# First operands of the down product in a two-level Strassen SwiGLU: loads and splits moved to a list of steps

## The chip, the core and the metric

The kernel runs on one core of a Trainium2 chip. Five engines work on their own instruction queues: PE (TensorE, matrix products), DVE (VectorE, elementwise work), ACT (ScalarE, activations and copies), POOL (GpSimd) and SP (SyncE, which here only issues transfers). The metric is the device time of one execution in microseconds (us); times below are medians of several executions of the same kernel.

## The reference, cut to what matters

Two layers over a residual stream of 1024 positions by 1024 channels. Layer 0 mixes with a short gated convolution, layer 1 with dilated attention; after each stands a SwiGLU feed-forward block, and a norm ends the whole. The part that this case is about is the feed-forward block, which runs twice:

```python
h = rms_norm(x, ffn_norm[i])
x = x + (jax.nn.silu(h @ w_gate) * (h @ w_up)) @ w_down    # 1024 -> 2816 -> 1024, all float32
```

## The kernel before, in words

**Precision.** A float32 product is made of three matmuls on a reduced type: an operand t is split into a high part (ACT rounds it, line 138 for weights, line 518 for activations) and a low part, t minus the high part (DVE, line 139 or 519); then high times high, high times low and low times high are added up in PSUM (lines 526 to 528). So every operand costs one ACT instruction, one DVE instruction, and three matmuls per use. Splits of activations are made by `hi` (line 516): it issues the ACT instruction at once and hands back a function that issues the DVE instruction.

**Strassen.** Products are done by the Strassen-Winograd scheme: seven products numbered 1 to 7 in place of eight, in the order `WINOGRAD = (1, 2, 6, 5, 7, 3, 4)`, over sums of quarters of the operands. For gate and up, the weights come in units of 256 columns; even unit numbers are gate, odd ones are up, 22 units in all (0 to 21). In units from 5 on, the products 2 and 4 of an even and an odd unit are done together with a second Strassen level, as seven "deep" products with numbers above 10 (`DEEPER = 10`), run with the odd unit. A product of the first level (`mm`, line 521) is 12 matmuls on 512 columns; a deep product (`deeper`, line 607) is 12 matmuls on 256 columns, whose results DVE adds to saved tiles (line 536).

**The order of the units.** It is written out by hand in `unit_order`, as a list of pairs (unit, product). `products` (line 554) walks through it, does the product at place n, and then calls `filled(n)` (in `run`, line 777), where other work is hung in. The last thirteen places, 168 to 180, are

```python
(21, 1) (20, 3) (21, 6) (21, 5) (21, 7) (21, 11) (21, 12) (21, 15) (21, 16) (21, 3) (21, 17) (21, 13) (21, 14)
```

**What comes after.** A finished pair of units gives four tiles of the hidden activations. `store` writes the Strassen sums of nine such pairs to DRAM tiles `parts[q, m]` (pair q, product m). The down product (`down`, line 741) reads them back: it works on chunks of three pairs (c = 0, 3, 6), and per chunk twice (n = 0 and n = 4) through the seven products, each with two blocks of 9 matmuls on 512 columns (k = n and k = n + 2); after each block DVE adds the bank to the residual stream X (line 747). After the two blocks of a product it calls `next(feed, None)`.

**The feed.** For a chunk, `feed` (line 715) is a generator whose step for product m loads the three tiles `parts[c + k, m]` into half pages named `hin` (line 723, on SP's queue) and then splits the three tiles that the step before loaded (ACT line 518, DVE line 519), into pages named `b`. For the first chunk its steps run at the places 176 to 180 of the unit order (the condition on line 791, the call on line 792) and then in `down`, after its products 1, 2 and 6: so product 1 is loaded at place 176 and split at place 177, product 2 split at 178, 6 at 179, 5 at 180, and 7, 3 and 4 within the down product.

**Queues and buffers.** Each engine runs its instructions in the order of the program. SP issues all weight loads (`raw`, line 152), the `hin` loads and the loads of X from its spilled copy (line 713, `load_x`) in program order too, each as soon as its buffer is free. Weights are split some products ahead (`take`, `ensure`). Half pages (128x512) come from a pool of 20, pages (128x1024) from a pool of 41, and PSUM has 8 banks; a new tile gets the place that has been free for the longest time, and its first writer waits for the last reader of the tile before.

Of the kernel before, what the change touches and what calls it, by code (L numbers as in the profile page):

```python
# [29 lines left out]
WINOGRAD = (1, 2, 6, 5, 7, 3, 4)  # L30
DEEP, DEEPER = (2, 4), 10
# [63 lines left out]
def trunk(ctx: ExitStack, tc: tile.TileContext, x, gains_in, cwi, ck, cwo, wqkv, wo, relb,  # L95
          wg, wu, wd, oneh, ident, out):
    nc = tc.nc
# [11 lines left out]
    def half_page(name, dt=F32):  # L109
        return scope["pool"].tile([128, 512], dt, name=name, tag="half", bufs=scope["halves"])  # L110
# [34 lines left out]
    ops, made, op_state = [], {}, [0, 0]  # L145
# [13 lines left out]
    def ensure(upto):  # L159
        while op_state[0] < min(upto + 1, len(ops)):  # L160
            key = ops[op_state[0] + 1][0] if op_state[0] + 1 < len(ops) else None
            if key in sums_of:
                sums_of.pop(key)()
            made[op_state[0]] = ops[op_state[0]][1]()
            op_state[0] += 1
# [49 lines left out]
    def add_deep(unit, key, u, rows, upto):  # L215
# [27 lines left out]
        def early(op):  # L243
            w = op()
            run(*[sums_of(j, m) for j, m in enumerate(DEEP)])
            return w
# [105 lines left out]
    def run(*gens):  # L352
        for _ in zip(*gens):
            pass
        for g in gens:
            for _ in g:
                pass
# [6 lines left out]
    def both(w, ks, acts):  # L364
        banks = two_banks()
        run(product(w, ks, acts, banks))
        return banks
# [126 lines left out]
    class Strassen:  # L494
# [215 lines left out]
        def load_x(self, *ns):  # L710
            for n in ns:
                X[n] = page("x")
                nc.sync.dma_start(X[n], self.source[n])

        def feed(self, c):

            tiles = None
            for m in WINOGRAD + (None,):
                new = None
                if m:  # L720
                    new = [half_page("hin") for k in range(self.chunk)]
                    for k in range(self.chunk):
                        nc.sync.dma_start(new[k], self.parts[c + k, m])
                if tiles:
                    lows = [self.hi(last, k, t, nc.vector)
                            for k, t in enumerate(tiles)]
                    for lo in lows:
                        lo()
                tiles, last = new, m
                if m:  # L730
                    self.b[m] = [None] * self.chunk
                    yield

        def feed_last(self, fs=None):
            for f in fs or self.plain:
                t = page("hin")
                nc.sync.dma_start(t, self.plain[f])
                self.hid[f] = split(t)
                yield

        def down(self, c, n, feed):

            p, r = {}, {}
            later = {2: (1,), 6: (3,), 5: (4,), 7: (6,), 3: (5,), 4: (7,)}

            def add(n, h, b):
                nc.vector.tensor_tensor(out=X[n][:, half(h)], in0=X[n][:, half(h)], in1=b, op=ALU.add)  # L747

            for m in WINOGRAD:
                for k in (n, n + 2):  # L750
                    if m == 1:
                        p[k] = bank()
                    if m == 5:
                        r[k] = bank()
                    b = bank() if m == 2 else r[k] if m in (3, 5) else p[k]
                    self.mm((c, k), m, b, m in (1, 2, 5), 4)
                    add(k + (m in (5, 7, 4)), int(m in (6, 5, 7, 3)), b)
                next(feed, None)
                if c == n == 0:
                    self.load_x(*later.get(m, ()))  # L760
                    self.rest(m)
# [10 lines left out]
        def run(self, start, hooks={}):  # L772

            self.base = op_state[1]
            last = self.nu - 1

            def filled(n):
                start(n)
                if self.key != CONV:
                    self.now = n + 1  # L780
                    i = self.order.index((3, 4))
                    if n == i - 10:
                        prep.append(self.deepen(2))
                    if n == i - 1:
                        prep.append(self.deepen(4))
                    for p in prep:
                        next(p, None)
                if self.key == CONV:
                    self.below(n, last)
                else:  # L790
                    if self.order[n][0] == last and n >= self.at(last, DEEPER + 6) - self.base:
                        next(feed, None)
                    if self.order[n] == (last, DEEPER + 7):
                        self.load_x(0, 2)
                        ensure(self.at(last, DEEPER + 4) + 4)
                self.idle(n)

            prep = []
            if self.key == CONV:
                self.products(filled, hooks)  # L800
                self.first_tiles()
                return
            feed = self.feed(0)
            self.products(filled, hooks)
            for c in range(0, self.pairs, self.chunk):
                self.down(c, 0, feed)
                feed = self.feed(c + self.chunk) if c + self.chunk < self.pairs else self.feed_last()
                self.down(c, 4, feed)
            run(feed)


    class Conv(Strassen):
# [148 lines left out]
        def first_tiles(self):  # L961

            run(self.low)
            upper = self.halved(range(CO, KT))
            for n in range(KT):
                banks = two_banks()
                run(product(take(("co", 0, n), 2), range(CO), self.hid, banks))
                if n + 2 < KT:
                    self.load_x(n + 2)
                add_to_x(n, banks)  # L970
                self.step(4 if n < 2 else None)
                if n >= 3:
                    next(upper, None)
            run(upper)
            for f in range(CO):
                del self.plain[f]
# [876 lines left out]
```

## Time and profile before

| what | before |
|---|---|
| median of 3 executions (lowest, highest) | 2205.99 us (2205.42, 2206.07) |
| span of the profiled execution, first to last instruction | 2203.1 us |
| ACT busy | 1000.5 us (45%) |
| POOL busy | 170.7 us (8%) |
| transfers, mean over the span | 119 GB/s |

The profiled execution shows no time of its own beside its span; the span ends 2.9 us below the median of the others. The two feed-forward blocks reach their last unit at about 749 us and 1940 us of the span. The busy time of PE counts overlapped matmuls once; waits are idle times of an engine before an instruction, with what released it. In a row of the timeline the columns are the start, the length, the engine, the line, the operation, the tile written and the tiles read, the size and the count of merged instructions.

### The profile page before, as it was taken

How to read it: one execution, taken by the hardware profiler on the slowest of the kernel's cores; microseconds unless marked ns; L12 is line 12 of the kernel's file. 1: busy time of each engine (PE TensorE's matmuls, PEld its weight loads, DVE VectorE, ACT ScalarE, POOL GpSimd, SP SyncE). 2: the span in 40 equal slices, each digit the busy share in tenths (PEclk: the TensorE clock that was granted, in tenths of full speed). 3: DMA queues.
4: the chain of work that ended last, by engine and by line, in shares of the span. 5: the costliest groups of instructions: out<-in, count | busy, mean ns of one | idle time of the engine just before them, and what ended most of it. 6: DMA issues, size and time to landing. Idle time of an engine off the chain costs nothing. (4 is left out here: it accounts for less than half of the span.)

```text
span 2203.1 us, 30573 instructions
## 1 busy us (share of the span) xinstructions
PE 2138.2 (97%) x11138; PEld 1825.5 (83%) x11138; DVE 1752.9 (80%) x3229; ACT 1000.5 (45%) x1812; POOL 170.7 (8%) x224
## 2 busy tenths in 40 slices
PE   7899999999999999999999999998999999999998
PEld 6788888778888878878999998886778888888887
DVE  7797758988888798865677777866888888889886
ACT  6433426434444444445455455534544444454435
POOL 0000001100101000010111111112000101000000
PEclk9999999999999999999999999998999999999999
DMA  4122543223323384323333333446223233366432
GB/s 155 55 86 71 210 153 87 96 91 100 116 96 120 117 281 144 119 68 131 91 91 92 94 97 90 152 154 170 77 77 102 105 105 111 96 226 204 158 91 77
DMA packets 135345, 261.89 MB, mean 119 GB/s; under 512 B 48328, under 2 KB 59608, under 8 KB 135194
## 3 DMA queue, kind: packets, MB, share of 16 engines
q1 hardware_dynamic: 75978, 184.80, 26.3%
q0 software_dynamic: 18048, 52.03, 7.0%
q10 hardware_dynamic: 41168, 23.10, 3.5%
q8 instruction: 88, 1.44, 0.3%
q14 instruction: 63, 0.52, 0.1%
HBM read 187.31 MB, written 66.27 MB: 115 GB/s over the span
## 5 line engine op out<-in xcount | busy, mean ns | idle before, releaser
L526 PE MATMUL bank<-b,w 128*128 128x512 f32 x1784 | 704.6, 395 | 25.6 <-DVE part L536 6.4
L528 PE MATMUL bank<-b,w 128*128 128x512 f32 x1784 | 700.4, 393 | 8.9 <-DVE w L139 8.9
L527 PE MATMUL bank<-b,w 128*128 128x512 f32 x1784 | 701.4, 393 | 0.0
L526 PEld LDWEIGHTS bank<-b,w 128*128 128x128 f32 x1784 | 338.6, 190 | 102.6 <-ACT part L532 7.4
L528 PEld LDWEIGHTS bank<-b,w 128*128 128x128 f32 x1784 | 338.7, 190 | 84.2 <-DVE w L139 13.1
L527 PEld LDWEIGHTS bank<-b,w 128*128 128x128 f32 x1784 | 338.7, 190 | 69.2 <-issue 0.7
L138 ACT ACTIVATE w<-combo 128x512 fp32r<-128x512 f32 (+2 forms) x464 | 234.5, 534 | 281.5 <-DVE combo L186 275.5
L139 DVE TENSOR_TENSOR w<-combo,w 128x512 fp32r<-128x512 f32 (+2 forms) x464 | 260.9, 576 | 57.5 <-ACT w L138 55.2
L532 ACT ACTIVATE part<-bank 128x512 f32<-128x512 f32 x168 | 99.5, 593 | 269.7 <-PE bank L528 258.6
L139 DVE TENSOR_TENSOR w<-raw,w 128x512 fp32r<-128x512 f32 (+2 forms) x316 | 169.4, 561 | 15.6 <-ACT w L138 14.1
L536 DVE TENSOR_TENSOR part<-part,bank 128x256 f32<-128x256 f32 (+1 forms) x348 | 159.1, 488 | 26.4 <-PE bank L528 14.2
L138 ACT ACTIVATE w<-raw 128x512 fp32r<-128x512 f32 (+2 forms) x316 | 150.7, 519 | 46.0 <-PE bank L528 11.2
L747 DVE TENSOR_TENSOR x<-x,bank 128x512 f32<-128x512 f32 x168 | 114.6, 682 | 30.7 <-PE bank L528 30.7
L347 PE MATMUL bank<-w_hi,w 128*128 128x512 f32 (+1 forms) x320 | 121.3, 379 | 4.4 <-ACT w L138 4.4
L349 PE MATMUL bank<-w_hi,w 128*128 128x512 f32 (+1 forms) x320 | 119.3, 373 | 0.9 <-DVE w L139 0.9
L348 PE MATMUL bank<-w_lo,w 128*128 128x512 f32 (+1 forms) x320 | 119.0, 372 | 0.0
L459 DVE TENSOR_TENSOR x<-x,bank 128x512 f32<-128x512 f32 (+1 forms) x104 | 66.1, 643 | 65.6 <-PE bank L349 57.3
L186 DVE TENSOR_TENSOR combo<-raw 128x512 f32<-128x512 f32 (+1 forms) x160 | 103.2, 645 | 4.0 <-DMA raw<-in_conv_w_in 4.0
L347 PE MATMUL bank<-h_hi,w_hi 128*128 128x512 f32 x256 | 104.6, 408 | 0.0
L349 PE MATMUL bank<-h_hi,w_lo 128*128 128x512 f32 x256 | 100.2, 391 | 0.7 <-DVE w_lo L139 0.7
L348 PE MATMUL bank<-h_lo,w_hi 128*128 128x512 f32 x256 | 99.9, 390 | 0.0
L1130 ACT ACTIVATE part<-part 128x512 f32<-128x512 f32 x66 | 39.7, 628 | 107.5 <-DVE part L536 107.5
(252 smaller groups left out, 3842.7 us busy)
## 6 DMA issues: line engine op xcount, KB each, us to landing
hin<-part SPq DMA_DIRECT2D x126, 256.0 KB
raw<-in_ffn_w_gate SPq DMA_DIRECT2D x44, 512.0 KB
raw<-in_ffn_w_up SPq DMA_DIRECT2D x44, 512.0 KB
part<-sum POOLq DMA_DIRECT2D x72, 256.0 KB, 2.7
raw<-in_ffn_w_down SPq DMA_DIRECT2D x48, 384.0 KB
x<-spill SPq DMA_DIRECT2D x24, 512.0 KB
raw<-in_attn_w_qkv SPq DMA_DIRECT2D x24, 512.0 KB
raw<-in_conv_w_in SPq DMA_DIRECT2D x21, 512.0 KB
```

Source lines behind the costliest of these rows:

```text
L138: nc.scalar.activation(hi, src, AF.Copy)
L139: eng.tensor_tensor(out=lo, in0=src, in1=hi, op=ALU.subtract)
L186: eng.tensor_tensor(out=c, in0=a, in1=b, op=op)
L347: nc.tensor.matmul(b, whi[:, a], ahi[:, s], start=first, stop=False)
L348: nc.tensor.matmul(b, whi[:, a], alo[:, s], start=False, stop=False)
L349: nc.tensor.matmul(b, wlo[:, a], ahi[:, s], start=False, stop=last)
L526: nc.tensor.matmul(b, hi[:, a], bhi, start=start and k == 0, stop=False, skip_group_check=True)
L527: nc.tensor.matmul(b, hi[:, a], blo, start=False, stop=False, skip_group_check=True)
L528: nc.tensor.matmul(b, lo[:, a], bhi, start=False, stop=k == n - 1, skip_group_check=True)
L532: nc.scalar.activation(t, b, AF.Copy)
L536: nc.vector.tensor_tensor(out=t, in0=t, in1=b, op=ALU.add)
L747: nc.vector.tensor_tensor(out=X[n][:, half(h)], in0=X[n][:, half(h)], in1=b, op=ALU.add)
```

## The change

In the feed-forward blocks, `feed` is taken apart into two functions, `load(m)` and `made(m)` (the split), and the first chunk gets a list of 17 steps of its own, `feed_first`. Its steps run from place 168 of the unit order on, after the last unit's first product; 13 of them lie in the units, four after the products 1, 2, 6 and 5 of the first pass of the down product. A pair (l, s) in the list means: split product s, then load product l. The other chunks' order is as before.

```diff
+        def feeding(self, c):
+
+            tiles = {}
+
+            def load(m):
+                tiles[m] = [half_page("hin") for k in range(self.chunk)]
+                for k, t in enumerate(tiles[m]):
+                    nc.sync.dma_start(t, self.parts[c + k, m])
+
+            def made(m):
+                self.b[m] = [None] * self.chunk
+                lows = [self.hi(m, k, t) for k, t in enumerate(tiles.pop(m))]
+                for lo in lows:
+                    lo()
+
+            return load, made
+
         def feed(self, c):
 
-            tiles = None
-            for m in WINOGRAD + (None,):
-                new = None
+            load, made = self.feeding(c)
+            for m, last in zip(WINOGRAD + (None,), (None,) + WINOGRAD):
                 if m:
-                    new = [half_page("hin") for k in range(self.chunk)]
-                    for k in range(self.chunk):
-                        nc.sync.dma_start(new[k], self.parts[c + k, m])
-                if tiles:
-                    lows = [self.hi(last, k, t, nc.vector)
-                            for k, t in enumerate(tiles)]
-                    for lo in lows:
-                        lo()
-                tiles, last = new, m
+                    load(m)
+                if last:
+                    made(last)
                 if m:
-                    self.b[m] = [None] * self.chunk
                     yield
+
+        def feed_first(self):
+
+            load, made = self.feeding(0)
+            for loads, mades in ((1, 0), (0, 0), (2, 0), (0, 1), (0, 0), (0, 2), (0, 0), (6, 0), (0, 0), (0, 6), (5, 0),
+                                 (0, 0), (0, 0), (7, 5), (3, 7), (4, 3), (0, 4)):
+                if mades:
+                    made(mades)
+                if loads:
+                    load(loads)
+                yield
...
-                    if self.order[n][0] == last and n >= self.at(last, DEEPER + 6) - self.base:
-                        next(feed, None)
+                    if n >= self.order.index((last, 1)):
+                        next(feed)
...
-            feed = self.feed(0)
+            feed = self.feed_first()
```

Laid beside the order of the units, the splits of the first chunk move so:

| operands of product | split before, after place | split in the changed kernel, after place |
|---|---|---|
| 1 | 177, (21, 3) | 171, (21, 5) |
| 2 | 178, (21, 17) | 173, (21, 11) |
| 6 | 179, (21, 13) | 177, (21, 3) |
| 5 | 180, (21, 14) | down product 1 |
| 7 | down product 1 | down product 2 |
| 3 | down product 2 | down product 6 |
| 4 | down product 6 | down product 5 |

The loads stand at the places 168 (product 1), 170 (2), 175 (6) and 178 (5), and after down products 1 (7), 2 (3) and 6 (4); before, they stood at 176, 177, 178, 179, 180 and after down products 1 and 2.

## The prediction, made before the result was known

> **What bounds the kernel now.** I read the page first, then the busy times by stage around the last unit of the first layer (the two feed-forward blocks are called layers here), then the timelines of PE, DVE, ACT and SP there.
>
> ```profile
> span 2203.1 us, 30573 instructions
> ...
> PE 2138.2 (97%) x11138; PEld 1825.5 (83%) x11138; DVE 1752.9 (80%) x3229; ACT 1000.5 (45%) x1812; POOL 170.7 (8%) x224
> ```
>
> PE is busy for 97% of the span: only its waits and its slow stretches can be won. The stages (columns: stretch, its length, busy us of PE, PEld, DVE, ACT, POOL, granted PE clock, DMA share, GB/s):
>
> ```profile
> 740.00:768.00 28.00, 28.00 (x150) 24.24 (x150) 20.79 (x45) 13.45 (x30) 1.62 (x3) 1.00 0.34 112
> 768.00:776.00 8.00, 6.23 (x42) 5.54 (x40) 7.38 (x18) 5.95 (x14) 0.54 (x1) 1.00 1.01 347
> 776.00:784.00 8.00, 7.76 (x33) 6.69 (x34) 7.97 (x18) 4.00 (x8) 0.00 (x0) 0.79 1.04 403
> 784.00:792.00 8.00, 6.55 (x30) 5.12 (x29) 7.97 (x15) 4.20 (x10) 1.08 (x2) 1.00 0.96 328
> ```
>
> From 740 to 768 PE never waits and DVE idles for 28.00 - 20.79 = 7.2 us. From 768 to 792 it turns round: DVE is full, the transfers are full (share 0.96 to 1.04), PE waits, and from 776 to 784 its clock is 0.79. So DVE bounds this stage. PE's waits there, with releaser, us, count and longest, and the timeline rows that matter:
>
> ```profile
> PE bank L618 <- DVE part L536: 2.0, 1, 2.0
> PE bank L526 <- ACT b L518: 1.8, 2, 1.5
> PE bank L526 <- DVE x L747: 0.5, 1, 0.5
> ...
> 771.20 0.28 PE L618 MATMUL bank<-t,w 128*128 128x256 f32 x1
> ...
> 773.95 0.28 PE L621 MATMUL bank<-b,w 128*128 128x256 f32 x1
> 776.24 0.36 PE L618 MATMUL bank<-t,w 128*128 128x256 f32 x1 [2.01 <-DVE part L536]
> ...
> 778.21 0.63 PE L526 MATMUL bank<-b,w 128*128 128x512 f32 x1
> ...
> 789.11 0.47 PE L526 MATMUL bank<-b,w 128*128 128x512 f32 x1 [1.45 <-ACT b L518]
> ...
> 810.62 0.39 PE L527 MATMUL bank<-b,w 128*128 128x512 f32 x1
> ...
> 811.07 0.39 PE L526 MATMUL bank<-b,w 128*128 128x512 f32 x1
> 811.30 0.39 PE L527 MATMUL bank<-b,w 128*128 128x512 f32 x1
> ...
> 1967.48 0.36 PE L618 MATMUL bank<-t,w 128*128 128x256 f32 x1 [2.01 <-DVE part L536]
> ```
>
> The wait at 776.24 is the last deep product (21, 14), which adds to banks that DVE has yet to read. The first pass of the down product starts at 778.21 and the second at 811.07: 32.86 us for 14 blocks of 9 matmuls. Undisturbed a matmul takes (811.30 - 810.62) / 3 = 0.227 us, so 126 take 28.6: 4.3 us are lost there, 3.1 in waits and 1.2 at the slow clock. With the 2.0 before and 0.5 of slow clock in (21, 14), some 6.8 us per layer. The second layer shows the same wait (1967.48), so the ceiling of any cure is about 13.6 us, 0.6%.
>
> DVE's queue, which sets these waits:
>
> ```profile
> 753.17 0.69 DVE L139 TENSOR_TENSOR w<-combo,w 128x512 fp32r<-128x512 f32 x1
> ...
> 758.37 0.69 DVE L139 TENSOR_TENSOR w<-combo,w 128x512 fp32r<-128x512 f32 x1 [1.22 <-ACT w L138]
> ...
> 763.53 0.69 DVE L604 TENSOR_TENSOR c<-part,bank 128x512 f32<-128x512 f32 x1 [2.27 <-ACT part L532]
> ...
> 766.80 0.68 DVE L139 TENSOR_TENSOR w<-combo,w 128x512 fp32r<-128x512 f32 x1
> ...
> 770.07 0.75 DVE L536 TENSOR_TENSOR part<-part,bank 128x256 f32<-128x256 f32 x2
> 771.40 0.69 DVE L536 TENSOR_TENSOR part<-part,bank 128x512 f32<-128x512 f32 x1 [0.59 <-PE bank L528]
> 772.73 1.89 DVE L519 TENSOR_TENSOR b<-hin,b 128x512 fp32r<-128x512 f32 x3
> 774.54 1.22 DVE L139 TENSOR_TENSOR w<-raw,w 128x256 fp32r<-128x256 f32 x3
> 775.68 0.75 DVE L536 TENSOR_TENSOR part<-part,bank 128x256 f32<-128x256 f32 x2
> ...
> 788.28 0.68 DVE L747 TENSOR_TENSOR x<-x,bank 128x512 f32<-128x512 f32 x1
> ...
> 797.10 0.68 DVE L747 TENSOR_TENSOR x<-x,bank 128x512 f32<-128x512 f32 x1
> ...
> 804.11 0.69 DVE L747 TENSOR_TENSOR x<-x,bank 128x512 f32<-128x512 f32 x1
> ```
>
> A split of three tiles takes DVE 774.54 - 772.73 = 1.81 us. The split of product 1 (772.73) stands in front of the adds of (21, 17) at 775.68, for which (21, 14) waits. The first add of the down product comes at 788.28, though its block had long left PE, because three more splits stand before it; the third product accumulates into that bank and starts at 789.11. The row's "ACT b L518" had been done for microseconds, so the add was the releaser.
>
> **The change, part by part.** The count of splits and loads is the same; all of it is order.
>
> *Split of product 1, now after (21, 5).* On DVE it falls into the idle 2.27 us before 763.53: after the two weight splits of (21, 11) it runs from about 760.1 to 761.9, the other four follow until 763.3, and the row at 763.53 need not move. On ACT its three instructions stand in front of the weights of (21, 12) and (21, 15):
>
> ```profile
> 762.90 0.60 ACT L532 ACTIVATE part<-bank 128x512 f32<-128x512 f32 x1 [2.24 <-PE bank L528]
> ...
> 767.41 1.66 ACT L518 ACTIVATE b<-hin 128x512 fp32r<-128x512 f32 x3
> 768.97 1.13 ACT L138 ACTIVATE w<-raw 128x256 fp32r<-128x256 f32 x3
> ...
> 772.33 0.63 ACT L518 ACTIVATE b<-hin 128x512 fp32r<-128x512 f32 x1 [1.19 <-DMA hin<-part]
> ```
>
> Three take 1.66, less than the idle 2.24 before 762.90. Cost nothing; without the cover 1.8.
>
> *Splits of 2 (after (21, 11)) and 6 (after (21, 3)).* Both now stand before the adds of (21, 17), where before only product 1's did. From 766.80 on DVE has no idle but the 0.59 before 771.40. So these adds come 2 x 1.81 - 1.81 - 0.59 = 1.2 us later, at 776.9, and (21, 14) starts at 777.4. Part of its wait moves forward: (21, 17) accumulates into banks of (21, 16), whose adds move from 770.07 to 771.9, so it starts at 772.4 where PE was free at 771.2. Term: **+1.2 us per layer**.
>
> *What goes in return.* No split stands between there and the down product's first add, where 2, 6 and 5 stood: it comes at 788.28 + 1.2 - 3 x 1.81 = 784.1. From it to the add of the third product there were two splits before (797.10) and are two after (5, 7): 792.9; to that of the fifth product (804.11) three before, four after: 784.1 + 15.8 + 1.8 = 801.7. PE, through (21, 14) at 778.8 at the earliest (12 matmuls of half the width, 1.4 us) and then without waits at 0.227 x 18 = 4.1 us a product, begins the third product at 787.0 or later, the fifth at 795.1, the seventh at 803.3; each needs the add of two products before, done 0.7 after the times given: 784.8, 793.6, 802.4. It always comes first, in the end by 0.9 us. Term: **-3.1 us per layer**.
>
> *Clock.* A slow stretch costs 8.00 x (1 - 0.79) = 1.7 us. It came after a wait of 2.01; after slightly shorter waits elsewhere it did not:
>
> ```profile
> 412.53 0.50 PE L528 MATMUL bank<-b,w 128*128 128x512 f32 x1 [1.92 <-DVE w L139]
> ...
> 412.50:416.50 4.00, 3.97 (x17) 3.30 (x18) 3.96 (x8) 1.16 (x3) 0.00 (x0) 1.00 0.16 18
> 776.20:780.20 4.00, 3.96 (x17) 3.60 (x18) 3.97 (x9) 0.86 (x2) 0.00 (x0) 0.62 1.03 406
> ```
>
> The old wait was 776.24 - 773.95 = 2.3 start to start. The new one follows (21, 17) at 772.4 and (21, 13), 1.4 each, so 775.3: 777.4 - 775.2 (last start) = 2.2 at the most, which lies between the two rows. Bounds: 0.3 us won if the clock still falls (the stretch then covers less of PE's work), 1.7 if it doesn't. I take one of the two layers: **-1.0 per layer**. The Trainium skill, "TensorE: Matmul & The Clock Gate", Part 1, says that the clock is halved after at least one idle window of about 3.4 us, and that the window runs free of the kernel; by that no wait here would halve it. This trace differs: 0.62 after 2.01 us.
>
> *Loads.* In the last unit they now stand earlier in SP's queue:
>
> ```profile
> 751.33 5.09 SPq L152 DMA_DIRECT2D raw<-in_ffn_w_down  x2
> 756.60 9.96 SPq L723 DMA_DIRECT2D hin<-part  x6
> ```
>
> The first six took 9.96 us to issue, since each waited for a half page to come free. At place 168 a count of first and last uses finds 9 of 20 half pages free; the first three loads take three at once, other tiles six, and loads 4 to 6 wait for pages that DVE frees at 753.9 and 759.1 (the weight splits at 753.17 and 758.37) and at 760.7 (the first tile of split 1), in time for ACT at 764. Behind them waits one weight tile (751.33 before, 760.7 now), which ACT reads no sooner than among the three at 768.97. Loads 7 to 9 take the places in time that 4 to 6 had, and the next weight tile goes behind them, 384 KB or 1.0 us at 403 GB/s, within the full stage. Between nothing and +1.0 us per layer I take nothing, since the first two loads now lie in the stage with a share of 0.34.
>
> Sum per layer: +1.2 - 3.1 - 1.0 = -2.9; two layers -5.8. Against the profiled execution the span goes from 2203.1 to 2197.3; the median of the runs is 2.9 above the span, 2205.99, so 2200.2.
>
> **The rivals.**
> - *No slow stretch at all.* The row of 412.53 speaks for it, that of 776.24 against. Each layer wins 1.2 - 3.1 - 1.7 = -3.6: 2198.8. By the page of the Trainium skill named above (TensorE: Matmul & The Clock Gate, Part 1), waits this short would have this result.
> - *DVE stays the bound in the down product.* The last margin is 0.9 us; weights that land 1.0 late, with waits before (21, 17) longer than worked out, take back half: 2203.1.
> - *The change doesn't do what it says.* If the early loads get no half pages sooner than before, split 1 waits at the head of ACT's queue, the weights of (21, 12) and (21, 15) behind it and PE behind these; the won time comes back as waits there: 2206. The count of 9 free speaks against it.
> - *Slower: the late load of product 6.* Its split stands before the adds of (21, 17) and takes the place in the transfers that the second load had; of that the third tile, issued by 766.6, let ACT go at 772.33. DVE reaches the third low part at 775.1 (772.73 + 1.2 + 2 x 0.6), ACT would have it at 773.0: 2.1 us of slack. Beyond, each us delays (21, 14) by one; from 5.0 us late the gain of 2.9 is gone, and at 7.6 us late each layer loses 2.5: 2211.
>
> **How the numbers follow.** Forecast 2200.2: 0.42, with a range of its own from 2199 to 2201.5; no slow stretch, 2198.8: 0.18; DVE stays the bound, 2203.1: 0.20; nothing won, 2206: 0.12; slower, 2211: 0.08. The range 2197.8 to 2204.8 takes the first three, 0.80. A measurement of this kernel tells 0.2%, 4.4 us, from no change, so faster means below 2201.6: nearly all of the first two and little of the third, 0.60; slower 0.08; the rest 0.32.
>
> **What would show it.** Right: DVE's idle before the row at 763.53 is gone and a split stands there; (21, 17) waits about 1 us and (21, 14) starts about 1.2 later than 776.24; the first add of the down product lies near 784; no wait of PE from there to the second pass, which starts near 808 rather than 811.07, and the same in the second layer. Wrong: waits of ACT on transfers or half pages between 757 and 764, PE waits at (21, 12) or (21, 15), a third tile of product 6 that ACT gets after 775, or PE waits for L747 that stay.

## The result, and the profile after

| | before | changed kernel |
|---|---|---|
| median (lowest to highest) | 2206.2 us (2203.79 to 2210.65), 20 executions | 2202.75 us (2197.22 to 2204.01), 20 executions |
| ratio, 95% interval | | 0.9978 [0.9971, 0.9984] |
| predicted | | 2200.2 us (2197.8 to 2204.8) |
| span of the profiled execution | 2203.1 us | 2202.2 us |

The change wins 0.22%, 3.5 to 6.4 us by the interval. The ratio is not that of the two medians, which lie 3.45 us apart (0.9984, the upper end of the interval). The sign and the range held; the median lies 2.55 us above the forecast. It also lies above 2201.6, below which the prediction would have called the kernel faster (0.60); yet with 20 executions of each kernel the whole interval lies below 1.

The profiled execution of the changed kernel reached its last unit 1.22 us later than that of before, for reasons that lie far ahead of the change: its matmuls are that much late from about 100 us of the span on (the rows below show the start of (21, 11)). So places are compared from there on: the **way** is the time from the first matmul of (21, 11) to the first of the down product's second pass. PE's timeline in the kernel before, both layers (the end of the first, 811.07, stands in the prediction):

```profile
762.70 0.28 PE L618 MATMUL bank<-b,w 128*128 128x256 f32 x1
...
1953.94 0.28 PE L618 MATMUL bank<-b,w 128*128 128x256 f32 x1
...
2002.33 0.39 PE L526 MATMUL bank<-b,w 128*128 128x512 f32 x1
```

The same of the changed kernel, with every row between 768 and 779 that has a wait:

```profile
763.92 0.28 PE L618 MATMUL bank<-b,w 128*128 128x256 f32 x1
...
770.56 0.50 PE L528 MATMUL bank<-b,w 128*128 128x512 f32 x1 [0.26 <-DVE w L139]
...
773.65 0.36 PE L618 MATMUL bank<-t,w 128*128 128x256 f32 x1 [0.51 <-DVE part L536]
...
778.58 0.35 PE L618 MATMUL bank<-t,w 128*128 128x256 f32 x1 [1.84 <-DVE part L536]
...
810.23 0.39 PE L526 MATMUL bank<-b,w 128*128 128x512 f32 x1
...
1955.19 0.28 PE L618 MATMUL bank<-b,w 128*128 128x256 f32 x1
...
2001.50 0.39 PE L526 MATMUL bank<-b,w 128*128 128x512 f32 x1
```

The way was 48.37 and 48.39 us in the two layers and is 46.31 in both: 2.07 won per layer, 4.1 in all, which is what the interval holds.

The profiled span is only 0.9 us shorter. Beside the 1.22 us of its late start, this execution was slower between the two ways: from the end of the first to the start of the second it took 1955.19 - 810.23 = 1144.96 us, where the kernel before took 1142.87. In all nine profiles of kernels with a changed list this stretch is 1.4 to 3.8 us longer than in the one profile of before, nearly all of it between about 1450 and 1565 us of the span, far from the change. Were these 2.1 us a cost of the change, its ratio would be 0.9991, which the interval excludes; so the one profile of before seems to have been short there by chance. Why is not shown.

The releasers of PE's waits from 740 to 820 (in all, count, longest):

```profile
PE bank L618 <- DVE part L536: 2.4, 2, 1.8
PE bank L528 <- DVE w L139: 0.3, 1, 0.3
```

The two rows of before on banks of L526, 2.3 us of waits within the down product (3.1 from start to start), are gone. What remains stands ahead of it: the wait at (21, 14), 2.01 before and 1.84 now, with a new one of 0.51 at (21, 17) and 0.26 at (21, 3). VectorE's queue shows why (line 767 is the old 747):

```profile
761.20 1.90 DVE L519 TENSOR_TENSOR b<-hin,b 128x512 fp32r<-128x512 f32 x3
...
764.75 0.69 DVE L604 TENSOR_TENSOR c<-part,bank 128x512 f32<-128x512 f32 x1 [0.32 <-ACT part L532]
...
768.02 1.89 DVE L519 TENSOR_TENSOR b<-hin,b 128x512 fp32r<-128x512 f32 x3
...
775.08 1.89 DVE L519 TENSOR_TENSOR b<-hin,b 128x512 fp32r<-128x512 f32 x3
776.88 1.22 DVE L139 TENSOR_TENSOR w<-raw,w 128x256 fp32r<-128x256 f32 x3
778.03 0.74 DVE L536 TENSOR_TENSOR part<-part,bank 128x256 f32<-128x256 f32 x2
...
785.21 0.68 DVE L767 TENSOR_TENSOR x<-x,bank 128x512 f32<-128x512 f32 x1
...
794.03 0.67 DVE L767 TENSOR_TENSOR x<-x,bank 128x512 f32<-128x512 f32 x1
...
802.85 0.67 DVE L767 TENSOR_TENSOR x<-x,bank 128x512 f32<-128x512 f32 x1
```

The idle 2.27 ahead of L604 has shrunk to 0.32: product 1's split (761.20) is in there. The splits of 2 (768.02) and 6 (775.08) stand ahead of the adds of (21, 17) at 778.03, and none stands between these and the first add of the down product, 785.21 (783.99 on before's scale, where it was 788.28). The last two rows are the first adds of the third and the fifth product.

The clock did not follow the forecast. The stages from 776 to 792 (columns as in the prediction):

```profile
776.00:784.00 8.00, 6.16 (x30) 5.35 (x29) 7.97 (x19) 1.56 (x3) 0.54 (x1) 0.79 1.03 406
784.00:792.00 8.00, 8.00 (x37) 6.63 (x36) 7.97 (x16) 5.01 (x10) 0.54 (x1) 1.00 0.94 324
```

From 784 PE never waits, where it had been busy for 6.55 of 8.00 us. But from 776 to 784 the granted clock is 0.79 as before: the slow stretch still comes, and in the second layer too.

### The profile page after: what moved, and what is told of

Same layout as the page of the kernel before. It is cut to its first block, busy times and chain, and to the rows that moved or that the text cites. A ratio compares the mean times of both kernels' runs of the same rounds, so it can differ in the third digit from the quotient of the medians.

```text
span 2202.2 us, 30565 instructions
## 1 busy us (share of the span) xinstructions
PE 2135.8 (97%) x11138; PEld 1823.1 (83%) x11138; DVE 1752.6 (80%) x3229; ACT 1000.5 (45%) x1812; POOL 170.7 (8%) x224
## 5 line engine op out<-in xcount | busy, mean ns | idle before, releaser
L526 PE MATMUL bank<-b,w 128*128 128x512 f32 x1784 | 704.2, 395 | 21.8 <-DVE part L536 6.4
L526 PEld LDWEIGHTS bank<-b,w 128*128 128x128 f32 x1784 | 338.2, 190 | 96.5 <-ACT part L532 8.2
```

The lines of the kernel that those rows point to most:

```text
L526: nc.tensor.matmul(b, hi[:, a], bhi, start=start and k == 0, stop=False, skip_group_check=True)
```

## The experiments

All of them change only the list in `feed_first`, and so the places of loads and splits; nothing of the computation is left out. The list is written in pairs (load, split): one for each place from 168 to 180, then one after each of the down product's first products.

**One part alone: product 1 early, the rest as late as before.**

```diff
-((1, 0), (0, 0), (2, 0), (0, 1), (0, 0), (0, 2), (0, 0), (6, 0), (0, 0),
- (0, 6), (5, 0), (0, 0), (0, 0), (7, 5), (3, 7), (4, 3), (0, 4))
+((1, 0), (0, 0), (0, 0), (0, 1), (0, 0), (0, 0), (0, 0), (0, 0), (0, 0),
+ (2, 0), (6, 2), (5, 6), (7, 5), (3, 7), (4, 3), (0, 4), (0, 0))
```

> Product 1 is loaded and split as in the changed kernel; products 2, 6, 5, 7, 3 and 4 are split as late as in the kernel before. Theory (what counts is how many splits stand on VectorE's queue ahead of each add that TensorE waits for): no split stands ahead of the adds of (21, 17) any more, so the wait of 2.0 us at (21, 14) is gone in both layers; but 2, 6 and 5 still stand ahead of the first add of the down product, so its third product waits some 3.3 us for that add. The second pass starts 0.2 to 1.9 us earlier per layer than before (0.2 if the clock falls after the new wait): 2202.4 to 2205.8, between the two kernels. Rival (the wait at (21, 14) and the slow clock behind it are the whole loss, and product 1 early is the whole gain): 2.0 + 1.7 us per layer, 2198.8, below the changed kernel.

Measured: 2203.14 us, ratio 0.9984 [0.9975, 0.9993]; the way is 46.68 and 46.73. PE's timeline has the wait at (21, 14) down to 0.20, and the one at the third down product, 1.45 in the kernel before, is 3.01. The second fence has VectorE's timeline: the split of 2, first of the three in the queue, and the add that PE waits for.

```profile
774.69 0.36 PE L618 MATMUL bank<-t,w 128*128 128x256 f32 x1 [0.20 <-DVE part L536]
...
787.56 0.61 PE L526 MATMUL bank<-b,w 128*128 128x512 f32 x1 [3.01 <-ACT b L518]
```

```profile
774.79 1.89 DVE L519 TENSOR_TENSOR b<-hin,b 128x512 fp32r<-128x512 f32 x3
...
786.73 0.68 DVE L767 TENSOR_TENSOR x<-x,bank 128x512 f32<-128x512 f32 x1
```

The theory holds: with the three splits of 2, 6 and 5 still ahead of the add at 786.73, PE is stopped there instead of at (21, 14). The rival falls, since a layer wins 1.7 us and not 3.7. What is won is one split: the add comes 786.73 - 762.96 = 23.77 us after (21, 11), where it came after 788.28 - 762.70 = 25.58, which is 1.81 less. In the down product the waits merely lie in another place: one of 3.0 us (3.2 from start to start), where the kernel before had three of together 2.3 (3.1). The profile puts that wait down to "ACT b", which had been done long before; the matmul starts 0.8 us after the add's row. The slow stretch went along, from (21, 14) to behind the new wait, as the stages from 776 to 792 show:

```profile
776.00:784.00 8.00, 8.00 (x38) 6.65 (x38) 7.97 (x17) 3.13 (x6) 0.77 (x2) 1.00 0.82 286
784.00:792.00 8.00, 4.99 (x16) 3.66 (x15) 7.97 (x16) 4.56 (x10) 0.31 (x1) 0.79 0.98 350
```

**The other part alone: 1, 2 and 6 as late as before; 5, 7, 3 and 4 later.**

```diff
+((0, 0), (0, 0), (0, 0), (0, 0), (0, 0), (0, 0), (0, 0), (0, 0), (1, 0),
+ (2, 1), (6, 2), (5, 6), (0, 0), (7, 5), (3, 7), (4, 3), (0, 4))
```

> Products 1, 2 and 6 are loaded and split where the kernel before has them; 5, 7, 3 and 4 each one down product later, as in the changed kernel. Theory: the wait of 2.0 us at (21, 14) and the slow clock behind it stay, but one split fewer stands ahead of the first add of the down product, and the waits there shrink from 3.1 us to about 1.2: 1.9 us per layer, 2202.4, as much as the whole change. Rival (the early loads and splits of 1, 2 and 6 are what wins): no change from before, 2206.

Measured: 2203.45 us, 0.9986 [0.9977, 0.9995]; the way is 46.57 and 46.58, 1.8 less than before, against 1.9 expected. No load or split is earlier here than in the kernel before, and nearly the whole gain of the changed kernel is there. The first add of the down product comes 23.77 us after (21, 11), as in the run above: again one split fewer stands ahead of it. The two parts win 1.69 and 1.80 us alone, 3.5 together, and the changed kernel, which has both, won only 2.07; the next run shows where the rest is. One thing was not expected: the wait of 2.01 at (21, 14) halved the clock in the second layer and not in the first. The stages of two windows of the first layer and two of the second:

```profile
772.98:776.40 3.42, 1.97 (x14) 1.92 (x15) 3.42 (x9) 0.46 (x1) 0.00 (x0) 1.00 1.01 376
776.40:779.81 3.41, 3.41 (x16) 2.81 (x15) 3.38 (x9) 0.56 (x2) 0.00 (x0) 1.00 0.91 301
1964.23:1967.64 3.41, 1.41 (x12) 1.23 (x12) 3.41 (x9) 2.22 (x4) 0.00 (x0) 1.00 1.03 396
1967.64:1971.05 3.41, 3.41 (x13) 2.93 (x12) 3.38 (x7) 0.00 (x0) 0.00 (x0) 0.50 1.00 379
```

And yet the way is the same in both layers. PE's waits for the down product's adds tell how, first layer, then second:

```profile
PE bank L526 <- ACT b L518: 2.1, 3, 1.2
...
PE bank L526 <- ACT b L518: 0.8, 2, 0.5
```

Where the clock fell, PE waited 1.3 us less: as long as PE would have to wait for VectorE's add anyway, a slow stretch costs nothing.

**The splits of the changed kernel, the loads only one step ahead.**

```diff
+((0, 0), (0, 0), (1, 0), (0, 1), (2, 0), (0, 2), (0, 0), (0, 0), (6, 0),
+ (0, 6), (0, 0), (0, 0), (5, 0), (7, 5), (3, 7), (4, 3), (0, 4))
```

> All splits stand exactly where the changed kernel has them; each load stands only one step ahead of its split. Theory (the order of the splits on VectorE sets the time, and the loads have slack): within 1 us of the changed kernel, 2202 to 2204. Rival (the loads well ahead are the gain): ScalarE waits for the transfers at the splits of 1, 2 and 6, the weights behind it come late, and the time goes back to 2206 or above.

Measured: 2201.89 us, 0.9969 [0.9959, 0.998]. In the first layer the way is 46.33, as in the changed kernel to 0.02: the distance of the loads is worth nothing. (The median lies 0.1 below the expected range.) In the second layer it is 44.80:

```profile
763.34 0.28 PE L618 MATMUL bank<-b,w 128*128 128x256 f32 x1
...
809.67 0.39 PE L526 MATMUL bank<-b,w 128*128 128x512 f32 x1
...
1955.11 0.28 PE L618 MATMUL bank<-b,w 128*128 128x256 f32 x1
...
1999.91 0.39 PE L526 MATMUL bank<-b,w 128*128 128x512 f32 x1
```

The order of the work is the same in both; the clock is not. The stages show three windows of each layer:

```profile
771.38:774.79 3.41, 2.89 (x20) 2.37 (x19) 3.38 (x9) 3.10 (x8) 0.00 (x0) 1.00 1.04 408
774.79:778.21 3.42, 1.59 (x14) 1.42 (x13) 3.42 (x9) 0.00 (x0) 0.54 (x1) 1.00 0.97 367
778.21:781.62 3.41, 3.41 (x15) 3.22 (x15) 3.38 (x10) 0.55 (x2) 0.00 (x0) 0.50 1.05 414
1962.63:1966.04 3.41, 2.88 (x18) 2.27 (x17) 3.38 (x10) 1.44 (x4) 0.00 (x0) 1.00 0.98 384
1966.04:1969.46 3.42, 1.95 (x17) 1.75 (x15) 3.42 (x8) 1.46 (x4) 0.54 (x1) 1.00 1.02 398
1969.46:1972.87 3.41, 3.04 (x19) 2.81 (x20) 3.38 (x9) 0.03 (x1) 0.00 (x0) 1.00 1.04 406
```

The slow stretches of one execution all begin on one grid of 3.413 us, and these windows are cut on it. In the first layer the wait of 1.83 lies in one window (3.42 - 1.59 idle), and the next window has half the clock; in the second the grid cuts the wait in 1.47 and 0.37, and the clock stays full. So **the slow stretch costs 46.33 - 44.80 = 1.53 us** here, where PE no longer waits for VectorE behind it. With a full clock the way is 48.39 - 44.80 = 3.59 us shorter than before, about the 3.5 of the two parts.

**Product 6 split two places later, behind (21, 13).** This takes one of the two splits from ahead of the adds of (21, 17); it ran twice.

```diff
-... (6, 0), (0, 0), (0, 6), (5, 0), (0, 0), (0, 0), ...
+... (6, 0), (0, 0), (0, 0), (5, 0), (0, 6), (0, 0), ...
```

> The changed kernel with one difference: product 6 is split behind (21, 13), two places later, so that one split, not two, stands ahead of the adds of (21, 17). Theory: these adds come 1.8 us earlier than in the changed kernel, (21, 14) waits some 0.2 to 0.5 us, the clock doesn't fall there, and the first add of the down product keeps its time; the second pass starts 4.4 us earlier per layer than before: about 2197.5 to 2199, the best of all. If only the slow clock stays all the same: 2201. Rival (the time lost in VectorE's queue is only moved, into waits of the down product on product 6's low parts or on its adds): 2202 to 2203, as the changed kernel.

> The same kernel as six_behind again, beside the changed kernel on one chip. Theory (the split of 6 ahead of the adds of (21, 17) costs 1.8 us at (21, 14), and without it no slow stretch falls there): 3 to 4.5 us below the changed kernel, and no slow stretch in the last unit of either layer. Rival (the difference between the two was the drawing of the slow stretches in those executions alone): the same time as the changed kernel.

Measured: 2198.01 us, 0.9963 [0.9951, 0.9975], and 2197.25 us, 0.9955 [0.9941, 0.9969]; the way is 44.05 to 44.09 in all four layers. PE's timeline and its stage from 776 to 784:

```profile
763.26 0.28 PE L618 MATMUL bank<-b,w 128*128 128x256 f32 x1
...
776.11 0.35 PE L618 MATMUL bank<-t,w 128*128 128x256 f32 x1
...
807.31 0.39 PE L526 MATMUL bank<-b,w 128*128 128x512 f32 x1
```

```profile
776.00:784.00 8.00, 7.99 (x42) 6.80 (x42) 7.93 (x17) 2.40 (x5) 1.08 (x2) 1.00 1.01 387
```

(21, 14) starts 776.11 - 763.26 = 12.85 us after (21, 11), where it was 778.58 - 763.92 = 14.66 in the changed kernel: 1.81 less, the length of one split. PE is busy for 7.99 of 8.00 us and its clock is full. A layer wins 2.2 us over the changed kernel. 1.53 of them are the slow stretch. The start that is 1.81 earlier gives the other 0.7; the rest of it is lost again further on, where VectorE, still full, lets PE wait at the fifth and sixth down products. The rival, that the drawing of slow stretches alone makes the difference, falls by the ways: against the 44.80 with a full clock a layer is still 0.7 shorter. The first add of the down product comes no later for it:

```profile
784.55 0.68 DVE L767 TENSOR_TENSOR x<-x,bank 128x512 f32<-128x512 f32 x1
```

That is 21.29 us after (21, 11), as in the changed kernel (785.21 - 763.92).

**The changed kernel again**, beside the last one:

> The changed kernel again. Theory (the wait of 1.8 us before (21, 14) halves the clock when it falls into one window of the throttle's grid, and not when it is cut by the grid, which lies differently in each execution): the way from (21, 11) to the second pass of the down product is 46.3 us with a slow stretch behind the wait and 44.8 without, layer by layer; the median 2201 to 2203. Rival (with the early loads the wait always halves it): 46.3 in both layers.

Measured: 2199.85 us over 5 executions, 0.9966 [0.9953, 0.9979]. In its profiled execution the clock fell in both layers and the way was 46.31 and 46.30, so this run did not tell the theory from its rival; the second layer of the kernel with late loads had. Its median is below the expected 2201 to 2203 and lower than the 2202.75 of 20 executions, but the intervals of the two ratios overlap. The last kernel, run beside it, is 2.6 us faster, short of the 3 to 4.5 that were expected, and these two intervals overlap as well: it is the ways, not the times of five executions each, that tell the two kernels apart.

**Both parts, but 2 and 6 not early.**

```diff
+((1, 0), (0, 0), (0, 0), (0, 1), (0, 0), (0, 0), (0, 0), (0, 0), (2, 0),
+ (6, 0), (5, 2), (0, 6), (0, 0), (7, 5), (3, 7), (4, 3), (0, 4))
```

> The edits of one_early and later_only together: product 1 split early, 2 and 6 where the kernel before has them, 5, 7, 3 and 4 one down product later. Theory: no wait at (21, 17) and (21, 14), two splits ahead of the first add, which comes 1.8 us earlier than in one_early, at 22.0 us after (21, 11); the third down product waits for it until 22.8, and the way to the second pass is 44.3 to 44.8 us, 3.6 to 4.1 less than before: 2198 to 2199, within 1 us of six_behind, so that the early split of 2 is worth next to nothing. Rival (2 has to be early too, since else VectorE is behind all through the down product): 45.5 us or more, 2200.5 or above.

Measured: a way of 44.75 and 44.77, within what was expected, and 0.7 more than with 2 early, so that the early split of 2 is worth 1.4 us in both layers and not next to nothing. Against the changed kernel a layer wins 1.5, though both splits stand late: PE waits only 0.2 us at (21, 14), and no slow stretch falls in the last unit of either layer. The median of 9 executions is 2201.67 us, 0.9966 [0.9956, 0.9976], above the 2198 to 2199 expected and among the rival's times (2200.5 or above); the rival's way of 45.5 or more is not what was measured. The ways account for 7.2 us against before, a ratio of 0.9967, which the measured one meets. Beside it the kernel before had a median of 2207.83, so that a part of the distance to the expected time is that of the two series.

**Product 6 as above, and 7, 3 and 4 one down product later each.**

```diff
-... (7, 5), (3, 7), (4, 3), (0, 4))
+... (7, 5), (3, 0), (4, 7), (0, 3), (0, 4))
```

> six_behind with the splits of 7, 3 and 4 one more down product later each (after products 6, 5 and 7), so that the adds of products 6 and 5 stand one split further ahead on VectorE's queue. Theory (what is left in the first pass are two waits of TensorE for adds, 0.2 us at the fifth product and 0.8 around the sixth): both go or shrink, the way from (21, 11) to the second pass falls from 44.1 to 43.1 to 43.6 us: 1 to 2 us below six_behind in all, 2195.5 to 2197. Rival (VectorE has no idle time there, so the waits only change from adds to low parts): 44.1 us, as six_behind.

Measured: 2196.06 us (2195.91 to 2198.11), 0.9952 [0.9938, 0.9965], the lowest median of all, though from another chip than the runs above, and its interval overlaps those of the kernel without this step. The way is 43.63 and 43.71, 0.4 less than without this step and just above what was expected. The waits for adds within the first pass are gone, but the rival is right in part: PE now waits for low parts. Its timeline and VectorE's where product 7 begins:

```profile
792.96 0.39 PE L526 MATMUL bank<-b,w 128*128 128x512 f32 x1
793.41 0.50 PE L527 MATMUL bank<-b,w 128*128 128x512 f32 x1
```

```profile
792.68 1.89 DVE L519 TENSOR_TENSOR b<-hin,b 128x512 fp32r<-128x512 f32 x3
```

The matmul on the first low part starts 0.45 after the one on the high part, where 0.227 is undisturbed, just as VectorE is done with that part, 0.7 after 792.68.

All of it together. From the ways of both layers follows a ratio (their difference to 48.37 + 48.39, over 2206.2); beside it the one that was measured:

| kernel | way, first and second layer | ratio from the ways | ratio measured |
|---|---|---|---|
| changed kernel | 46.31, 46.31 | 0.9981 | 0.9978 [0.9971, 0.9984] |
| the same again | 46.31, 46.30 | 0.9981 | 0.9966 [0.9953, 0.9979] |
| product 1 early alone | 46.68, 46.73 | 0.9985 | 0.9984 [0.9975, 0.9993] |
| 5, 7, 3, 4 later alone | 46.57, 46.58 | 0.9984 | 0.9986 [0.9977, 0.9995] |
| loads one step ahead | 46.33, 44.80 | 0.9974 | 0.9969 [0.9959, 0.998] |
| 6 behind (21, 13) | 44.05, 44.07 | 0.9961 | 0.9963 [0.9951, 0.9975] |
| the same again | 44.07, 44.09 | 0.9961 | 0.9955 [0.9941, 0.9969] |
| 2 and 6 not early | 44.75, 44.77 | 0.9967 | 0.9966 [0.9956, 0.9976] |
| 6 behind, 7, 3, 4 later | 43.63, 43.71 | 0.9957 | 0.9952 [0.9938, 0.9965] |

Nine intervals, eight of which hold the ratio from the ways; the ninth, of five executions, ends at 0.9979 where one profiled execution gives 0.9981, and an execution that escapes both slow stretches would be 3.1 us faster, 0.9967.

## Why the prediction was right, and where not

- *Split of product 1 into VectorE's idle time, at no cost*: right. The idle 2.27 became 0.32 and L604 kept its place (764.75 - 1.22 = 763.53).
- *+1.2 from the splits of 2 and 6 ahead of the adds of (21, 17)*: right. (21, 17) starts at 772.43 on before's scale (that is, less 1.22; predicted 772.4), (21, 14) at 777.36 (777.4). The 0.26 at (21, 3), whose low weights stand behind the split of 2, was not listed; it is contained in the late start of (21, 17).
- *-3.1 from the down product's waits*: right. The first add of the down product comes at 783.99 (784.1), those of the third and the fifth product at 792.81 and 801.63 (792.9 and 801.7). The margin of 0.9 for the last add is borne out where it was thinnest: in the second layer with late loads and a full clock, PE went through the down product's first pass without a wait, and the way was 44.80 us, 3.59 less than before; the terms 1.2 - 3.1 - 1.7 gave 3.6.
- *-1.0 from the clock*: this is the mis-sized term. The prediction took one slow stretch of the two layers to vanish. In the profiled execution neither did, nor in the second one; then the clock gives what the prediction had as its lower bound, 0.3, and the sum 1.2 - 3.1 - 0.3 = -2.2 per layer against 2.07 measured. The wrong idea was to judge by the length of the wait, with one layer of two as the even chance between the rows of 1.92 and 2.01. The new wait was 1.84 us of idle time, shorter than both, and the clock fell all the same. What counts in these places is where the grid cuts the wait. Of the 1.92 us at 412.53 in the kernel before, 1.30 lay in one window, and the clock stayed full; in the changed kernel's profile the same wait, 1.94 us, lay in one window whole, and from 414.04 to 417.45 the granted clock was 0.50. The starts of the two layers lie 1955.19 - 763.92 = 1191.27 us apart, 349 windows of 3.4133 us to within 0.02 (the period follows from slow stretches far apart in one trace: in the kernel before, those that begin at 29.62 and 1968.39 are 568 windows apart): where one layer's wait falls into one window, so does the other's. In the kernel with late loads the layers are 1191.77 apart, half a microsecond off the grid, and there they differed; in the changed kernel's second execution they were off it as well, and the clock fell in both all the same. The Trainium skill, "TensorE: Matmul & The Clock Gate", Part 1, says that the window runs free of the kernel, and these rows agree; it also asks for a whole idle window, and here 1.83 us of 3.41 were enough.
- *The slow stretch as a loss beside the waits* (1.2 of the 4.3 us lost in the first pass): a misreading, though the sum came out. The run with 5, 7, 3 and 4 later, whose down product waits for VectorE as that of before does, shows a stretch that costs nothing. It began to cost 1.53 only once the change had taken the wait behind it away. So the change made the clock matter, and then gave part of its gain to it: without the two slow stretches the ways would be 7.2 us shorter, not 4.1.
- *Loads at no cost*: right, and more than that: the early loads aren't needed. With one step of distance the way is the same.
- *The rivals.* That VectorE stays the bound in the down product, or that nothing is won, is refuted by PE's busy 8.00 of 8.00 us from 784 on; that product 6 comes late, by ScalarE's row for its third tile:

```profile
771.47 0.63 ACT L518 ACTIVATE b<-hin 128x512 fp32r<-128x512 f32 x1 [0.39 <-DMA hin<-part]
```

VectorE came to these splits at 775.08. "No slow stretch" did not come about in either profiled execution of the changed kernel, and in only one of the six layers of the three profiled executions that have its order of splits.

What the prediction did not see: its own term of +1.2 could be avoided. It took the places of the list as given and priced them; that product 6's split has no reason to stand ahead of the adds of (21, 17), since the first add of the down product comes equally early with it behind them, could have been read from the same rows.

## What to carry to other kernels

When an engine with a full queue feeds another, list for each wait the work that stands ahead of its releaser, and ask of each piece which of the waits it delays: with one part alone, PE no longer waited 2.0 us at (21, 14) but 3.0 at the next add that the splits delayed; for product 6 the place between both, behind the adds of (21, 17) and no further, won at both. Distance between a load and its use was worth nothing once the load was in time. A slow stretch of the clock that hides under a wait cost nothing here, and got its price when the wait went, so price it in the kernel after, not before.

## What the runs showed that was not expected

The clock's grid can explain part of the spread between executions of one kernel. In ten profiled executions each slow stretch starts on a grid of 3.413 us that lies differently in every execution. In the windows around the last unit of both layers, every window in which PE was idle for 1.82 us or more (1.82 to 3.01, ten cases) was followed by a slow one, and none in which it was idle for 1.47 or less; elsewhere in the kernel, outside of slow stretches, there are cases of both kinds between about 1.15 and 1.95. So for waits like those of the last unit the place on the grid decides; what else does in the cases elsewhere is not shown. The 20 executions of the changed kernel lie as far apart as 2197.22 and 2204.01 us; the two stretches of its last units would account for 3.1 of these 6.8 us, and no run shows how much is theirs. Not explained: in three executions PE had a slow stretch at about 967 to 972 us though the profile shows it busy throughout the window before.
